# Sink attention: reciprocal sums widened on VectorE and turned inside the heads' banks, output casts a step later; fewer, larger loads at the start

## The chip, the cores and the metric

The kernel runs on one core of a Trainium2 chip. The metric is device time of one execution in microseconds, the median of three runs. A core has TensorE (PE; its weight loads are shown apart as PEld), VectorE (DVE), ScalarE (ACT), GpSimd (POOL) and SyncE (SP), which here only issues DMAs. Each engine works through its own queue in order; engines wait for one another by semaphores.

## The reference

Two blocks run one after the other on 256 tokens of width 1024, all in fp32. The first block has a gated feed-forward layer, a mixing layer with two kinds of attention, and a second feed-forward layer. The second block has two layers, each attention and then a feed-forward layer: the first with sliding-window attention with sinks (the *sink layer*), the second with stick-breaking attention. The sink layer is where most of the change lies; its core, cut:

```python
s = jnp.einsum('bqkgd,bskd->bkgqs', qb, kb).astype(jnp.float32) * scale
s = jnp.where(valid, s, -jnp.inf)
sink_col = jnp.broadcast_to(sink_logit, s.shape[:-1] + (1,))
p = jax.nn.softmax(jnp.concatenate([s, sink_col], axis=-1), axis=-1)[..., :-1]
o = jnp.einsum('bkgqs,bskd->bqkgd', p.astype(vb.dtype), vb)
```

So each query's exponentials are divided by their sum, the sink's own exponential included, over 16 heads of 64 features.

## The kernel before

Activations lie with features on partitions and 256 tokens along the free dimension. Every large matrix product is made of three matmuls on rounded halves: a high part (a cast to fp32r, `h`) and a low part (the rest, `l`), for the weights and for the activations. Weights come in blocks of 16 tiles of 128x128 (1 MB) into `raw`; ScalarE casts four tiles at a time to `wh` (L218), VectorE subtracts to `wl` (L226), and `W.step` lets one such quarter go after every four tiles of matmuls (`mm3`, L278 to L280). All other work is written as generators in a list of hooks: `pump()` lets each hook go one step and then calls `W.step`. So a step is twelve matmuls of 256 columns and whatever the hooks put into the queues in between; while an out projection waits for heads that are not ready, `pump()` is called with no matmuls in between.

**The start.** SP issues eight pairs of loads (L300, L302): a chunk of x (128 KB, called x0 to x7 here) and four weight tiles (256 KB, w0 to w7), then the rest of the weights and the constants. For each pair, ScalarE makes `xgh` (L843), the square `sq` (L335) and the cast `wh`, VectorE the low parts `xgl` (L846) and `wl`, and TensorE runs twelve matmuls on it. Eight fp32 matmuls on ones (L315), two passes each, run before the first load is there.

**The sink layer.** `soft_heads` takes heads in pairs; `run_heads` keeps up to three pairs going and starts one every second step at most. In the sink layer a pair goes: step 0, scores on TensorE (L697) and masked minimum on VectorE (L709); step 1, four exponentials on ScalarE with their sums (L718); step 2, reciprocal of the 2x2 sums on VectorE (`rs`, L723) and its spread to 64 columns for each head on GpSimd (`rw`, L727); step 3, three transposes for each head (`turn`, L739, copied to `pt` by ScalarE, L741), then two transposes of `rw` and a copy (`over_features`, L756, `rf`, L759); step 5, values (`weigh`, L749), the product `y` with `rf` on VectorE (L795) and the cast to `yh` on ScalarE (L797); step 6, the low part `yl` on VectorE (L799); step 7, the pair is marked ready for the out projection. PSUM banks for all of this come from `at_ps`, four in turn; an allocation waits until the bank four before it has been read. Beside it `operand` normalizes and rotates q and k, with transposes (L1114), copies to `qT` (L1120) and several GpSimd operations for each.

Of the kernel before, what the change touches and what calls it, by code (L numbers as in the profile page):

```python
# [11 lines left out]
F32 = mybir.dt.float32  # L12
# [7 lines left out]
S = 256  # L20
DC = 8
# [143 lines left out]
def hybrid_two_block_kernel(ctx: ExitStack, tc: tile.TileContext, x, w, ada, vecs, rows, pos, consts,  # L165
                            masks, out):
    nc = tc.nc
# [9 lines left out]
    def nm(s):  # L177
        count[0] += 1
        return f"{s}_{count[0]}"
# [4 lines left out]
    def at_ps(shape):  # L184
        return pp.tile(shape, F32, tag="at", bufs=4, name=nm("at"))
# [74 lines left out]
    W = Stream()  # L260
# [22 lines left out]
    xT = xp.tile([128, DC, S], F32, name="xT")  # L283
# [12 lines left out]
    for i in range(2):  # L296
        W.raw[i] = wp.tile([128, 16, 128], F32, tag="raw", bufs=W.RAW, name=nm("raw"))
    W.loaded = 2
    for kc in range(DC):
        nc.sync.dma_start(xT[:, kc], x[:, kc * S:(kc + 1) * S])  # L300
        i, t = divmod(4 * kc, 16)
        nc.sync.dma_start(W.raw[i][:, t:t + 4], w[i, :, 128 * t:128 * t + 512].rearrange("p (t c) -> p t c", t=4))  # L302
    W.load(3, 4)
    W.load(W.RAW, 2)
    nc.sync.dma_start(V[:, 8:], vecs[:, 8:])
# [3 lines left out]
    ident = C[:, C_ID:C_ID + 128]  # L309
# [1 line left out]
    ones = cp.tile([128, 128], F32, name="ones")  # L311
    nc.vector.memset(ones, 1.0)
    warm = at_ps([128, 128])
    for _ in range(8):
        nc.tensor.matmul(warm, lhsT=ones, rhs=ones, start=True, stop=True)  # L315
    mean_col = cp.tile([128, 1], F32, name="mean_col")
    nc.vector.memset(mean_col, 1.0 / D)
# [333 lines left out]
    def pause(n):  # L651
        for _ in range(n):
            yield

    def soft_heads(pool, n_heads, n_parts, part, y_h, y_l, ready, sink=None, gate=lambda j: True,
# [6 lines left out]
        cut = 128 + (sink is not None)  # L662
# [5 lines left out]
        def one(c):  # L668

            js = (2 * c, 2 * c + 1)  # L670
# [12 lines left out]
            u, lo, sums = {}, {}, {}  # L683
            both = pool.tile([128, 2, 2], F32, tag="sm", bufs=6, name=nm("sm"))
# [7 lines left out]
            for g in range(n_parts):  # L692
                p = {j: at_ps([128, 384]) for j in js}
# [25 lines left out]
                                         bias=lo[j][:, 2 * g + tt:2 * g + tt + 1],  # L719
                                         scale=-1.0, accum_out=sums[j][:, tt:tt + 1])  # L720
            yield from pause(gaps[0])
            rs = pool.tile([128, 2, 2], F32, tag="rs", bufs=6, name=nm("rs"))
            nc.vector.reciprocal(rs, both)  # L723
            if sink is not None:
                wide_rs = [pool.tile([128, 2, 64], F32, tag="rw", bufs=6, name=nm("rw")) for _ in range(2)]
                for tt in range(2):
                    nc.gpsimd.tensor_copy(wide_rs[tt], rs[:, tt].unsqueeze(2).to_broadcast([128, 2, 64]))  # L727
            if sink is None:
                for j in js:
                    for tt, sl in ((0, slice(0, 128)), (1, slice(cut, cut + 256))):  # L730
# [4 lines left out]
            def turn(j, g):  # L735

                ps = at_ps([128, 384])
                for at, a in ((0, 0), (128, cut), (256, cut + 128)):
                    nc.tensor.transpose(ps[:, at:at + 128], u[j][:, g, a:a + 128], ident)  # L739
                pt = pool.tile([128, 384], F32, tag="pt", bufs=6, name=nm("pt"))  # L740
                nc.scalar.copy(pt, ps)  # L741
                return pt

            def weigh(g, pts):
                for i in range(2):
                    for j in js:
                        v = part(j, g)[2][i]
                        oh = o[64 * (j % 2):64 * (j % 2) + 64, 128 * i:]
                        nc.tensor.matmul(oh, lhsT=v, rhs=pts[j][:, 256 * i:256 + 128 * i], start=g == 0 and i == 0,  # L749
                                         stop=g == n_parts - 1 and i == 1)  # L750

            def over_features():

                ps = at_ps([128, S])
                for tt in range(2):
                    nc.tensor.transpose(ps[:, 128 * tt:128 * tt + 128], wide_rs[tt].rearrange("p h e -> p (h e)"),  # L756
                                        ident)
                t = pool.tile([128, S], F32, tag="rf", bufs=3, name=nm("rf"))
                nc.scalar.copy(t, ps)  # L759
                return t  # L760

            pts = None
            for g in range(n_parts + 1):
                while not values():
                    yield
                if pts is not None:
                    if g == 1:
                        o = (at_ps if sink is not None else mm_ps)([128, S])
                    weigh(g - 1, pts)
                if g < n_parts:  # L770
                    if last is not None and pending:
                        pending.pop(0)()
                    pts = {j: turn(j, g) for j in js}
                    if sink is not None:
                        rf = over_features()
                    if last is not None:
                        break
                    yield from pause(gaps[2])
            if last is not None:
# [7 lines left out]
                o = None  # L787
# [4 lines left out]
                return  # L792
            if sink is not None:
                y = pool.tile([128, S], F32, tag="y", bufs=3, name=nm("y"))
                nc.vector.tensor_mul(y, o, rf)  # L795
                o = y
            nc.scalar.copy(y_h[:, c], o)  # L797
            yield
            nc.vector.tensor_sub(y_l[:, c], o, y_h[:, c])  # L799
            yield  # L800
            ready.add(c)

        pending, last = [], n_heads // 2 - 1 if merged else None
        return run_heads(n_heads // 2, one, gate, spacing, most)


# [34 lines left out]
    for d in range(DC):  # L841
# [7 lines left out]
        i, t = divmod(4 * d, 16)  # L849
# [25 lines left out]
    with ExitStack() as mix:  # L875
# [73 lines left out]
        with tc.tile_pool(name="merge", bufs=1) as gp:  # L949
# [5 lines left out]
            for d in range(DC):  # L955
# [6 lines left out]
                for kc in range(4):  # L962
                    t = 4 * (d % 4) + kc
                    mm3(pb, bh[:, t], bl[:, t], ybh[:, kc], ybl[:, kc], kc == 0, kc == 3)
                for kc in range(2):
                    t = 2 * d + kc
# [200 lines left out]
    with ExitStack() as mix:  # L1167
# [122 lines left out]
        name = "wqkv_b_2"  # L1290
# [74 lines left out]
```

## Time and profile before

| | |
|---|---|
| median of three runs | 1174.76 us (1174.7 to 1174.78) |
| profiled execution | 1174.54 us |
| its span | 1172.7 us |
| TensorE busy | 1160.4 us (99%) |
| VectorE busy | 946.5 us (81%) |
| ScalarE busy | 627.3 us (53%) |
| GpSimd busy | 125.3 us (11%) |
| DMA | 251.72 MB, mean 215 GB/s |

Times inside the profile count from the start of its span. The start of the kernel is 0 to 17 us; the heads of the sink layer run from about 605 to 672 us. Busy shares are means over the whole span; what an edit is worth is read from the stretch it lies in, and there from which wait ends last.

### The profile page before, as it was taken

What the parts mean: (1) busy time and instruction counts of PE and PEld (TensorE: products, weight loads), DVE (VectorE), ACT (ScalarE), POOL (GpSimd) and SP (SyncE); (2) the same over time, 40 slices, a digit from 0 to 9 for tenths busy, and PEclk for the clock granted to TensorE, in tenths of its full rate; (3) what the DMA queues carried; (4) which work ended last, traced back from release to release, by engine and by line L of the source; (5) the groups of instructions that cost most, each with busy time, mean ns of one, the idle gap of its engine ahead of it and who ended that gap; (6) DMA issues with size and microseconds to landing.
All of it is one profiled execution on the core that took longest, in us unless ns stands there. A gap on an engine that the chain in (4) does not pass through costs nothing.

```text
span 1172.7 us, 24635 instructions
## 1 busy us (share of the span) xinstructions
PE 1160.4 (99%) x9762; PEld 1129.9 (96%) x9762; DVE 946.5 (81%) x1991; ACT 627.3 (53%) x1344; POOL 125.3 (11%) x174
## 2 busy tenths in 40 slices
PE   9999999999999999999999999999999999999998
PEld 8999999999899999999997899999999999999998
DVE  7999987565667999999876699999969677888652
ACT  6545544455546554554467765554448666555531
POOL 2000011120202200001256220000110002000000
PEclk9999999999999999999999999999999999999999
DMA  8887756534334777876551277777654436765450
GB/s 318 325 299 276 269 210 209 213 113 176 114 139 149 259 275 306 334 277 233 180 187 72 83 284 296 307 270 278 249 191 149 164 122 215 258 215 181 170 200 20
DMA packets 45762, 251.72 MB, mean 215 GB/s; under 512 B 5328, under 2 KB 7888, under 8 KB 22224
## 3 DMA queue, kind: packets, MB, share of 16 engines
q1 hardware_dynamic: 45072, 248.78, 58.1%
q8 instruction: 77, 1.26, 0.4%
q10 hardware_dynamic: 576, 1.38, 0.4%
q14 instruction: 37, 0.30, 0.1%
HBM read 249.09 MB, written 1.05 MB: 213 GB/s over the span
## 4 chain that ended last, share of the span: by engine, by line
PE 90%; DVE 5%; ACT 2%; POOL 1%; issue 1%; DMA 0%; SPq 0%; DVEq 0%; ACTq 0%; POOLq 0%
PE mm L278 26%; PE mm L279 26%; PE mm L280 26%; DVE wl L226 2%; PE mm L594 1%; PE mm L596 1%; PE mm L595 1%; PE at L279 1%; PE at L280 1%; PE at L278 1%; PE at L697 1%; PE at L739 1%; ACT wells L718 1%; PE mm L749 1%; PE at L1233 1%
## 5 line engine op out<-in xcount | busy, mean ns | idle before, releaser
L218 ACT CAST wh<-raw 128x512 fp32r<-128x512 f32 (+1 forms) x749 | 420.4, 615 | 241.9 <-issue 117.6
L226 DVE TENSOR_TENSOR wl<-raw,wh 128x512 fp32r<-128x512 f32 (+1 forms) x749 | 502.4, 704 | 52.5 <-ACT wh L218 51.8
L278 PE MATMUL mm<-xgh,wh 128*128 128x256 f32 (+1 forms) x1712 | 486.1, 284 | 0.3 <-DVE sh L1037 0.2
L280 PE MATMUL mm<-xgh,wl 128*128 128x256 f32 (+1 forms) x1712 | 482.9, 282 | 0.0
L279 PE MATMUL mm<-xgl,wh 128*128 128x256 f32 (+1 forms) x1712 | 482.1, 282 | 0.0
L278 PEld LDWEIGHTS mm<-xgh,wh 128*128 128x128 f32 x1712 | 322.9, 189 | 4.3 <-issue 3.6
L279 PEld LDWEIGHTS mm<-xgl,wh 128*128 128x128 f32 x1712 | 324.0, 189 | 0.0
L280 PEld LDWEIGHTS mm<-xgh,wl 128*128 128x128 f32 x1712 | 323.1, 189 | 0.0
L279 PE MATMUL mm<-al,wh 128*128 128x256 f32 x704 | 197.0, 280 | 0.0
L278 PE MATMUL mm<-ah,wh 128*128 128x256 f32 x704 | 196.8, 280 | 0.0
L280 PE MATMUL mm<-ah,wl 128*128 128x256 f32 x704 | 196.4, 279 | 0.0
L278 PEld LDWEIGHTS mm<-ah,wh 128*128 128x128 f32 x704 | 132.3, 188 | 0.1
L279 PEld LDWEIGHTS mm<-al,wh 128*128 128x128 f32 x704 | 132.1, 188 | 0.0
L280 PEld LDWEIGHTS mm<-ah,wl 128*128 128x128 f32 x704 | 131.8, 187 | 0.0
L338 POOL TENSOR_TENSOR ssq<-ssq,sq 128x256 f32<-128x256 f32 x56 | 47.1, 846 | 669.0 <-ACT sq L335 668.1
L429 DVE SCALAR_TENSOR_TENSOR acc<-ada,cs,acc 128x1024 f32<-128x1024 f32 x84 | 107.6, 1281 | 1.1 <-DMA ada<-in_ada 0.5
L335 ACT ACTIVATE sq<-xT 128x256 f32<-128x256 f32 x49 | 19.9, 411 | 80.8 <-DVE xT L555 72.3
L491 DVE TENSOR_TENSOR tu<-mm,rB 128x256 f32<-128x256 f32 x80 | 33.5, 419 | 20.6 <-PE mm L280 20.5
L504 ACT CAST ah<-a 128x256 fp32r<-128x256 f32 x88 | 35.3, 405 | 23.3 <-DVE a L502 16.7
L497 ACT ACTIVATE sg<-tg,bb 128x256 f32<-128x256 f32 x44 | 22.3, 508 | 32.4 <-DVE bb L495 31.8
L506 DVE TENSOR_TENSOR al<-a,ah 128x256 fp32r<-128x256 f32 x88 | 36.6, 420 | 1.9 <-ACT ah L504 1.9
L280 PE MATMUL at<-xgh,wl 128*128 128x256 f32 (+1 forms) x128 | 36.7, 287 | 0.8 <-DVE wl L226 0.6
(227 smaller groups left out, 1552.6 us busy)
## 6 DMA issues: line engine op xcount, KB each, us to landing
raw<-in_w SPq DMA_DIRECT2D x183, 1024.0 KB, 5.4
ada<-in_ada SPq DMA_DIRECT2D x96, 512.0 KB, 4.8
raw<-in_w SPq DMA_DIRECT2D x12, 256.0 KB, 5.3
xT<-in_x SPq DMA_DIRECT2D x8, 128.0 KB, 4.6
raw<-in_w SPq DMA_DIRECT2D x2, 512.0 KB, 8.2
out<-xT SPq DMA_DIRECT2D x8, 128.0 KB, 2.1
M<-in_masks ACTq DMA_DIRECT2D x1, 768.0 KB, 4.3
Mstick<-in_masks ACTq DMA_DIRECT2D x1, 386.0 KB, 3.0
```

Source lines behind the costliest of these rows:

```text
L218: nc.scalar.copy(h[:, part], self.raw[i][:, part])
L226: engine.tensor_sub(l[:, part], self.raw[i][:, part], h[:, part])
L278: nc.tensor.matmul(ps, lhsT=lh, rhs=rh, start=start, stop=False)
L279: nc.tensor.matmul(ps, lhsT=lh, rhs=rl, start=False, stop=False)
L280: nc.tensor.matmul(ps, lhsT=ll, rhs=rh, start=False, stop=stop)
L335: nc.scalar.activation(t, src, AF.Square, scale=scale)
L338: nc.gpsimd.tensor_add(self.ssq, self.ssq, t)
L429: nc.vector.scalar_tensor_tensor(self.acc, raw, self.cs[:, kc:kc + 1], self.acc, op0=ALU.mult, op1=ALU.add)
L491: nc.vector.tensor_mul(tu, ps[1][:, :S], norm.r)
L497: nc.scalar.activation(sg, tg, AF.Silu, bias=bb[:, 0:1] if shift else 0.0)
L504: nc.scalar.copy(ah[:, c], a)
L506: nc.vector.tensor_sub(al[:, c], a, ah[:, c])
```

## The change

At the start, the eight pairs of loads become five: chunks 0 and 1 singly, then 2 and 3, 4 and 5, 6 and 7 together, x and weights alike. Ten instead of eight matmuls on ones run ahead. In the sink layer one VectorE reciprocal reads the 2x2 sums with a broadcast and writes them 64 columns wide for each head and half (`wide_rs`, 128x256); GpSimd's two copies are gone. `turn_two` puts a head's three transposes and one transpose of `wide_rs` into one 512-column bank and copies the bank at once; `rf` is the last quarter of these copies. The cast to `yh` moves from step 5 to step 6, right ahead of the low part. Other attention layers keep their path.

```diff
-    for kc in range(DC):
-        nc.sync.dma_start(xT[:, kc], x[:, kc * S:(kc + 1) * S])
+    for kc, n in ((0, 1), (1, 1), (2, 2), (4, 2), (6, 2)):
+        nc.sync.dma_start(xT[:, kc:kc + n], x[:, kc * S:(kc + n) * S].rearrange("p (c s) -> p c s", c=n))
         i, t = divmod(4 * kc, 16)
-        nc.sync.dma_start(W.raw[i][:, t:t + 4], w[i, :, 128 * t:128 * t + 512].rearrange("p (t c) -> p t c", t=4))
+        nc.sync.dma_start(W.raw[i][:, t:t + 4 * n],
+                          w[i, :, 128 * t:128 * (t + 4 * n)].rearrange("p (t c) -> p t c", t=4 * n))
...
-    for _ in range(8):
+    for _ in range(10):
         nc.tensor.matmul(warm, lhsT=ones, rhs=ones, start=True, stop=True)
...
-            rs = pool.tile([128, 2, 2], F32, tag="rs", bufs=6, name=nm("rs"))
-            nc.vector.reciprocal(rs, both)
-            if sink is not None:
-                wide_rs = [pool.tile([128, 2, 64], F32, tag="rw", bufs=6, name=nm("rw")) for _ in range(2)]
-                for tt in range(2):
-                    nc.gpsimd.tensor_copy(wide_rs[tt], rs[:, tt].unsqueeze(2).to_broadcast([128, 2, 64]))
+            if sink is None:
+                rs = pool.tile([128, 2, 2], F32, tag="rs", bufs=6, name=nm("rs"))
+                nc.vector.reciprocal(rs, both)
+            else:
+                wide_rs = pool.tile([128, 2, 2, 64], F32, tag="rw", bufs=4, name=nm("rw"))
+                nc.vector.reciprocal(wide_rs, both.unsqueeze(3).to_broadcast([128, 2, 2, 64]))
...
-            def over_features():
-
-                ps = at_ps([128, S])
-                for tt in range(2):
-                    nc.tensor.transpose(ps[:, 128 * tt:128 * tt + 128], wide_rs[tt].rearrange("p h e -> p (h e)"),
-                                        ident)
-                t = pool.tile([128, S], F32, tag="rf", bufs=3, name=nm("rf"))
-                nc.scalar.copy(t, ps)
-                return t
+            def turn_two():
+
+                pt = pool.tile([128, 2, 512], F32, tag="pt2", bufs=3, name=nm("pt2"))
+                for j in js:
+                    ps = at_ps([128, 512])
+                    for at, a in ((0, 0), (128, cut), (256, cut + 128)):
+                        nc.tensor.transpose(ps[:, at:at + 128], u[j][:, 0, a:a + 128], ident)
+                    nc.tensor.transpose(ps[:, 384:512], wide_rs[:, j % 2].rearrange("p h e -> p (h e)"), ident)
+                    nc.scalar.copy(pt[:, j % 2], ps)
+                return {j: pt[:, j % 2, :384] for j in js}, pt[:, :, 384:512]
...
-                    pts = {j: turn(j, g) for j in js}
-                    if sink is not None:
-                        rf = over_features()
+                    if sink is None:
+                        pts = {j: turn(j, g) for j in js}
+                    else:
+                        pts, rf = turn_two()
...
-                nc.vector.tensor_mul(y, o, rf)
+                nc.vector.tensor_mul(y.rearrange("p (t q) -> p t q", t=2), o.rearrange("p (t q) -> p t q", t=2), rf)
                 o = y
-            nc.scalar.copy(y_h[:, c], o)
-            yield
+                yield
+                nc.scalar.copy(y_h[:, c], o)
+            else:
+                nc.scalar.copy(y_h[:, c], o)
+                yield
             nc.vector.tensor_sub(y_l[:, c], o, y_h[:, c])
```

## Rows read from the trace of the kernel before

**Rows 1.** The page, busy time of each engine, share of the span, instructions

```profile
PE 1160.4 (99%) x9762; PEld 1129.9 (96%) x9762; DVE 946.5 (81%) x1991; ACT 627.3 (53%) x1344; POOL 125.3 (11%) x174
```

**Rows 2.** What TensorE waited for, whole span: us in total, times, longest

```profile
PE at L756 <- POOL rw L727: 2.0, 4, 0.9
...
PE at L739 <- ACT qT L1120: 0.7, 1, 0.7
```

**Rows 3.** Timeline of TensorE at the start: start us, us, instruction, [idle before <-releaser]

```profile
1.05 3.69 PE L315 MATMUL at<-ones 128*128 128x128 f32 x16 [1.05 <-DVE mhalf L319]
...
5.50 0.38 PE L278 MATMUL at<-xgh,wh 128*128 128x256 f32 x1 [0.76 <-ACT wh L218]
...
14.82 0.38 PE L280 MATMUL at<-xgh,wl 128*128 128x256 f32 x1 [0.39 <-DVE wl L226]
```

**Rows 4.** Timeline of SP's DMA issues at the start: issues of w2 and w3

```profile
3.06 0.43 SPq L302 DMA_DIRECT2D raw<-in_w  x1
...
4.01 0.43 SPq L302 DMA_DIRECT2D raw<-in_w  x1
```

**Rows 5.** DMA issues, KB each, median us to landing: w2, w3, block 3's halves

```profile
raw<-in_w SPq DMA_DIRECT2D x1, 256.0 KB, 5.2
...
raw<-in_w SPq DMA_DIRECT2D x1, 256.0 KB, 5.3
...
raw<-in_w SPq DMA_DIRECT2D x2, 512.0 KB, 8.2
```

**Rows 6.** Timeline of ScalarE at the start: the casts of w2 and w3

```profile
8.30 0.62 ACT L218 CAST wh<-raw 128x512 fp32r<-128x512 f32 x1 [0.59 <-DMA raw<-in_w]
...
9.55 0.60 ACT L218 CAST wh<-raw 128x512 fp32r<-128x512 f32 x1
```

**Rows 7.** Stretches: length, busy (instructions) of PE, PEld, DVE, ACT, POOL, PEclk, DMA, GB/s

```profile
5.00:10.00 5.00, 4.14 (x28) 3.56 (x29) 3.47 (x7) 4.36 (x11) 1.94 (x3) 1.00 0.90 301
10.00:15.00 5.00, 4.61 (x37) 4.32 (x37) 4.86 (x7) 4.55 (x12) 3.55 (x5) 1.00 0.89 246
```

**Rows 8.** VectorE's groups, 598 to 672 us: busy us, mean ns, idle before

```profile
L1100 DVE TENSOR_TENSOR ht<-at,R 128x256 f32<-128x256 f32 x9 | 3.4, 419 | 2.5 <-ACT hsq L1099 1.8 <-POOL rw L727 0.7
...
L1103 DVE TENSOR_SCALAR hss<-hss 128x4 f32<-128x4 f32 x9 | 1.5, 171 | 0.3
L723 DVE RECIPROCAL rs<-sm 128x4 f32<-128x4 f32 x8 | 1.4, 176 | 9.4 <-ACT wells L718 9.3
...
L1036 DVE COPY shb<-mm 128x1 f32<-128x1 f32 x8 | 1.2, 150 | 0.4 <-PE mm L280 0.4
```

**Rows 9.** ScalarE's groups of the same stretch

```profile
L741 ACT COPY pt<-at 128x384 f32<-128x384 f32 x16 | 6.8, 479 | 2.3 <-PE at L739 2.3
...
L797 ACT CAST yh<-y 128x256 fp32r<-128x256 f32 x8 | 3.2, 406 | 9.8 <-DVE y L795 9.8
L759 ACT COPY rf<-at 128x256 f32<-128x256 f32 x8 | 3.1, 385 | 0.0
```

**Rows 10.** Timelines of TensorE and of ScalarE around 640 us

```profile
638.38 0.91 PE L739 MATMUL at<-C,wells 128*128 128x128 f32 x6
...
643.65 0.48 PE L756 MATMUL at<-C,rw 128*128 128x128 f32 x2
...
639.67 0.40 ACT L797 CAST yh<-y 128x256 fp32r<-128x256 f32 x1 [1.40 <-DVE y L795]
...
641.08 0.41 ACT L718 ACTIVATE wells<-wells,lo 128x129 f32<-128x129 f32 x1
...
642.85 0.63 ACT L1120 ACTIVATE qT<-at 128x256 f32<-128x256 f32 x2
```

**Rows 11.** The same two timelines around 660 us

```profile
656.93 0.87 PE L739 MATMUL at<-C,wells 128*128 128x128 f32 x6
...
662.13 0.33 PE L756 MATMUL at<-C,rw 128*128 128x128 f32 x1 [0.42 <-POOL rw L727]
...
657.50 0.41 ACT L797 CAST yh<-y 128x256 fp32r<-128x256 f32 x1 [1.73 <-DVE y L795]
```

## The prediction

> **What bounds the kernel now.** I read the busy shares first: TensorE is busy for 1160.4 of 1172.7 us, VectorE for 81%, ScalarE for 53% [rows 1]. The chain of work that ended last says the same: nearly all of it is matmuls. So time can only be won or lost where TensorE itself stands still, and a stall added or removed there is passed on whole, because the matmuls behind it follow one another without slack. Third, the list of what TensorE waited for, over the whole span [rows 2]: the sink layer stands in it with 2.0 us in four waits for GpSimd's copy rw, and 0.7 us for a bank that ScalarE still reads. Last the timeline of the start, where the waits are for the first casts and low parts [rows 3]. These are fractions of a microsecond each; no large gain is on offer, and 0.2% (2.35 us) is about what a measurement of this kernel can tell from no change.
>
> **The profiled execution** took 1174.54 us, span 1172.7 us; the median of the runs shown is 1174.76, 0.22 us more. I make the sum against 1174.54 and add the 0.22 at the end.
>
> **Part 1, the loads at the start.** Up to the second weight piece nothing changes: x0, w0, x1, w1 are issued in the same order, and the first real matmul waits for the cast of w0 and starts at 5.50 [rows 3]. Two more warm-up matmuls: the 16 passes of eight take 3.69 us from 1.05, 0.23 a pass [rows 3]; four more end 0.92 us later at that price, at 5.66. The hole in front of the first matmul is 0.76 us [rows 3], so they cost between 0 and 0.16 us; I take 0, since the 3.69 holds the start and the tail of a row of passes too, and a further pass costs less than 0.23.
>
> The third pair is where it decides. Today w2 (256 KB) is issued at 3.06 [rows 4] and lands 5.2 us later [rows 5], at 8.26; ScalarE's cast of it starts at 8.30 after 0.59 us of waiting for that DMA [rows 6]. From there the path is tight: VectorE, which makes the low parts, is busy for 4.86 of the 5 us from 10 to 15 [rows 7], and TensorE waits for it at the end of that row of splits again (0.39 us before 14.82) [rows 3]. So a later w2 moves everything behind it, one for one. After the change x2 and x3 come as one transfer of 256 KB and w2 and w3 as one of 512 KB, issued when x2 and w2 are. The cast of w2 then waits for the last byte of w3. Bounds: not before w2 lands today, 8.26 (gain excluded: more bytes stand ahead of the same event), and not later than w3 lands today, 4.01 + 5.3 = 9.31 [rows 4, 5], because up to there the queue carries the same 1536 KB and today's is issued a microsecond later. That is +0 to +1.05 us. I take +0.7, nearer to the upper end, since the slowest of the 16 engines sets a landing and the same bytes lie before it. Behind it nothing new is late: w3 is then there; w4 to w7 come in steps of 768 KB for two pairs, and at the 301 GB/s of 5 to 10 us [rows 7] that is 2.6 us, against 2.5 us that ScalarE takes for two pairs (8.30 to 9.55 for one [rows 6]). Fewer issues also free SP's queue: sixteen issues become ten. This moves block 2 and the small constants forward, which TensorE does not wait for today, so it is worth nothing.
>
> **Part 2, the sink layer.** Per pair of heads (eight pairs) the change removes a reciprocal of four elements (176 ns [rows 8]), two GpSimd copies and a 256-column ScalarE copy (385 ns [rows 9]); it adds a VectorE reciprocal of 256 elements and makes two copies 512 columns wide instead of 384. The transposes stay eight. The copies: 384 columns take 479 ns, 256 take 385 [rows 9], so 0.73 ns a column and 0.57 us for 512; two of them 1.15 against 2 x 0.479 + 0.385 = 1.34 us. ScalarE wins 0.19 us a pair. The wide reciprocal is not in this trace. Lower bound: it streams like the other 128x256 operations, 0.42 us (ht, 419 ns [rows 8]). Upper bound: a copy of one element takes 150 ns and the reciprocal of four 176 [rows 8]; if those 26 ns are all due to three more elements, 8.7 ns each, 256 take 0.18 + 252 x 8.7 = 2.4 us. Nearer is TENSOR_SCALAR on four elements, 171 ns [rows 8]: 5 ns over four is 1.2 ns each on top, and 0.73 us. I take 0.42, since an operation of the same size that is no reciprocal explains all but these 5 ns.
>
> The Trainium skill speaks against this step: its page "VectorE: DVE Perf Modes", section "First, the fixed hardware budget", says that the reciprocal is an iterative divide with a repeat count of 8. If that means eight passes for each element, the instruction would come out near the 2.4 us of the upper bound and the sum as in rival B; the four-element row, 5 ns above its neighbour, does not bear it out.
>
> What goes: TensorE's waits for rw, 2.0 us [rows 2]; the longest, 0.9, stands around 640, the last, 0.42, before 662.13 [rows 11], the others at the first and last pair. What takes their place: the reciprocal is queued on VectorE behind something new. Today the cast of y is queued on ScalarE at once behind y, and ScalarE stands waiting for it (1.40 us before 639.67 [rows 10], 1.73 before 657.50 [rows 11]). Afterwards cast and low part come in the next step together, ahead of the reciprocal of the pair two further on. On ScalarE the cast then lies behind that pair's four exponentials (1.77 us, 641.08 to 642.85 [rows 10]) and a weight cast or two qT copies; on VectorE the low part waits for the cast, and the reciprocal waits behind the low part.
>
> I follow it at the two places where TensorE has nothing else to do. *Around 640:* the transposes of that pair start at 638.38 [rows 10], or about 0.5 earlier with the first pairs' waits gone (637.9); ScalarE no longer waits for y, 0.6 until the first wide copy can start, 1.0 until the exponentials start, 1.8 for them, 0.6 for two qT copies [rows 10], 0.4 each for the cast, the low part and the reciprocal, 0.6 for the five transposes that are left, 5.8 in all: 643.7. Today the same transposes end at 644.13 (643.65 + 0.48 [rows 10]). Gain 0.4 us, of the 0.9 and 0.7 that stood there. *Around 660:* today 656.93 (transposes begin) to 662.46 is 5.5 us, the next matmul following at once [rows 11]. Afterwards the same terms hold, with one weight cast (0.6, as in [rows 6]) in place of the qT copies: 5.8 us. So 0.3 of the 0.4 goes back. Sum of the stage: -0.1 us. Its range: -2.0 (all waits for rw go and nothing replaces them) to +1.1 (the reciprocal at 0.73 in both places, 0.6 together, and a second weight cast of 0.6 ahead of the cast).
>
> The later cast itself costs the projection nothing: the pair's mark of readiness stays in the same step, and where the last pair's result is first used some 24 matmuls lie between.
>
> **Sum:** 1174.54 + 0.7 - 0.1 + 0.22 = 1175.4 us.
>
> **The rivals.**
> - *A, faster:* ScalarE, no longer waiting for y (9.8 us in the stage [rows 9]), runs so far ahead that the cast is done before VectorE asks for it; then the waits for rw (2.0) and for the qT bank (0.7) [rows 2] go, and the third load lands where w2 does: 1174.76 - 2.7 = 1172.1. It decides from the point where the cast of one pair ends before the exponentials two pairs on. Against it: these stand ahead of it in ScalarE's order. Chance 0.13.
> - *B, slower, the reciprocal iterates:* 2.4 instead of 0.42 us stands on the path at both places, 2 x 1.98 = 4.0 on top of the forecast: 1179.4. It decides from about 1.3 us an instruction. Against it: the four-element row. Chance 0.11.
> - *C, slower, the third load is late:* a 512 KB piece of this kernel has been seen to take 8.2 us to landing [rows 5]; from 3.06 that is 11.3, 3.0 later than today: 1174.76 + 3.0 - 0.1 = 1177.7. Against it: those pieces stood behind seven others. It decides from a landing 2.5 us later. Chance 0.07.
>
> **How the numbers follow.** Forecast 0.69, A 0.13, B 0.11, C 0.07. The forecast lies in the band of 1172.4 to 1177.1, so within 0.2% has 0.69, faster 0.13, slower 0.18. The forecast's own range is 1172.8 (0 and -2.0) to 1176.9 (+1.05 and +1.1). The range reaches towards A and takes in C: 1172.3 to 1177.8; B and about half of A, which lies just outside, are left out, 0.18 together.
>
> **What would show it.** The cast of w2 starts between 8.3 and 9.3, later than today, with a DMA named as what it waited for, and the row of splits behind it is later by as much. The 128x256 reciprocal takes 0.4 to 0.7 us. No TensorE wait names rw; new ones name the reciprocal, of up to 2 us before the last pair's transposes; VectorE's low part waits for the cast, up to 1.5 us each, and ScalarE's 9.8 us of waiting for y are gone. Wrong if w2 and w3 land at 8.3 or earlier, if the start gains, or if the transposes around 662 stand without a wait for the reciprocal.

## The result, and the profile after

The changed kernel takes **1185.36 us** (median of 4 runs, 1184.47 to 1187.48) against 1174.77 of before: a ratio of 1.0090, 95% interval 1.0078 to 1.0102. It is 10.6 us slower. The prediction was 1175.4 us with no measurable change; its range ended at 1177.8. The profiled execution took 1187.48 us, span 1185.7, the slowest of the four; the terms below that come from its trace are those of this execution. Of the later cast alone, one of the experiments below, one execution ran at a granted clock of 0.655 and took 1589 us; it is left out, and with it the only trace of that version.

The wide reciprocal stands in VectorE's groups of the sink layer, 598 to 690 us (line, engine, operation, shapes and count; busy us, mean ns; idle before), where [rows 8] had the four-element one, with the low part below it:

```profile
L728 DVE RECIPROCAL rw<-sm 128x256 f32<-128x256 f32 x8 | 14.0, 1748 | 3.2 <-ACT wells L719 3.0
...
L805 DVE TENSOR_TENSOR yl<-y,yh 128x256 fp32r<-128x256 f32 x8 | 3.9, 484 | 6.0 <-ACT yh L801 6.0
```

It takes 1748 ns, ten times the 176 of [rows 8] and four times what the sum put in. The low part waits 6.0 us for the cast. ScalarE's groups of the same stretch, for [rows 9]:

```profile
L761 ACT COPY pt<-at 128x512 f32<-128x512 f32 x16 | 9.0, 587 | 13.0 <-PE at L760 13.0
...
L801 ACT CAST yh<-y 128x256 fp32r<-128x256 f32 x8 | 3.2, 404 | 2.6 <-DVE y L798 2.6
```

The 512-column copy is at 587 ns as worked out (0.57), and the wait for y fell from 9.8 to 2.6 us. But ScalarE stands 13.0 us for TensorE's transposes of rw, because TensorE itself stands ahead of them (2.3 us for transposes in [rows 9]). What TensorE waited for, whole span, for [rows 2]:

```profile
PE at L760 <- DVE rw L728: 8.7, 4, 3.3
PE at L278 <- ACT wh L218: 1.6, 1, 1.6
```

The four waits for GpSimd's copies, 2.0 us, became four waits for VectorE's reciprocal, 8.7 us, the longest 3.3 us, ahead of 650.60. All four in the timeline of TensorE (start us, us, instruction, [idle before <-releaser]), with the transposes just ahead of the longest:

```profile
626.47 0.33 PE L760 MATMUL at<-C,rw 128*128 128x128 f32 x1 [1.87 <-DVE rw L728]
...
643.94 0.33 PE L760 MATMUL at<-C,rw 128*128 128x128 f32 x1 [0.73 <-DVE rw L728]
...
646.72 0.55 PE L759 MATMUL at<-C,wells 128*128 128x128 f32 x3
650.60 0.33 PE L760 MATMUL at<-C,rw 128*128 128x128 f32 x1 [3.33 <-DVE rw L728]
...
672.12 0.47 PE L760 MATMUL at<-C,rw 128*128 128x128 f32 x1 [2.79 <-DVE rw L728]
```

ScalarE's timeline ahead of 650.60:

```profile
644.31 0.59 ACT L761 COPY pt<-at 128x512 f32<-128x512 f32 x1 [1.70 <-PE at L760]
645.28 0.59 ACT L761 COPY pt<-at 128x512 f32<-128x512 f32 x1 [0.39 <-PE at L760]
645.77 0.41 ACT L719 ACTIVATE wells<-wells,lo 128x129 f32<-128x129 f32 x1
...
647.54 0.39 ACT L801 CAST yh<-y 128x256 fp32r<-128x256 f32 x1
```

and VectorE's:

```profile
645.06 0.42 DVE L798 TENSOR_TENSOR y<-at,pt 128x256 f32<-128x256 f32 x1
647.96 0.92 DVE L805 TENSOR_TENSOR yl<-y,yh 128x256 fp32r<-128x256 f32 x1 [2.48 <-ACT yh L801]
648.80 1.74 DVE L728 RECIPROCAL rw<-sm 128x256 f32<-128x256 f32 x1
```

Read from below: the transposes of rw wait for a reciprocal of 1.74 us, which stands behind the low part, which stands 2.48 us for a cast that lies behind four exponentials although its input y is there at 645.48. That is the order the prediction followed, with another duration at its end.

A second loss was not in the prediction at all. Stretches of the changed kernel (length; busy and instructions of PE, PEld, DVE, ACT, POOL; granted clock; DMA share; GB/s):

```profile
627.00:630.00 3.00, 3.00 (x16) 3.00 (x15) 2.73 (x9) 2.47 (x6) 2.69 (x7) 0.50 0.00 0
651.00:654.00 3.00, 3.00 (x15) 2.02 (x14) 0.65 (x3) 2.25 (x5) 0.00 (x0) 0.50 0.03 5
672.00:677.50 5.50, 5.38 (x25) 5.38 (x26) 1.96 (x5) 2.00 (x4) 0.00 (x0) 0.50 0.01 3
```

and the first of them in the kernel before:

```profile
627.00:630.00 3.00, 3.00 (x31) 2.50 (x27) 2.58 (x14) 1.89 (x7) 1.88 (x3) 1.00 0.00 0
```

The granted clock is at 0.50 (1.2 GHz, the lower of its two levels) in the three stretches, in each of which TensorE had stood for rw just before or at its start (1.87 us before 626.47, 3.33 before 650.60, 2.79 before 672.12). TensorE is busy in them, but with half the instructions: 16 in 3 us instead of 31. Before, the clock is at 1.00 there. At the start the clock fell too in this execution: 0.76 over 10 to 15 us, where [rows 7] have 1.00.

Instructions that both kernels have start 2.0 us later at 600 us (the start's share), 13.15 later at 690 (the sink layer's share is 11.1), and 13.15 later to the end: nothing else differs.

At the start, two rows of ScalarE's timeline: the high part of x2, and the cast of w2 that answers to [rows 6]:

```profile
8.43 0.51 ACT L849 ACTIVATE xgh<-xT,V 128x256 fp32r<-128x256 f32 x1 [1.61 <-DMA xT<-in_x]
...
10.10 0.62 ACT L218 CAST wh<-raw 128x512 fp32r<-128x512 f32 x1 [0.85 <-DMA raw<-in_w]
```

and TensorE's, for [rows 3]:

```profile
5.34 0.55 PE L278 MATMUL at<-xgh,wh 128*128 128x256 f32 x1
...
10.77 0.39 PE L278 MATMUL at<-xgh,wh 128*128 128x256 f32 x1 [1.57 <-ACT wh L218]
```

The cast of w2 moved from 8.30 to 10.10 us. ScalarE stood for the merged x2 and x3 first, 1.61 us, which the prediction did not count, and then for the merged weights. The two more warm-up matmuls cost nothing (first real matmul at 5.34, 5.50 before).

### The profile page after: what moved, and what is told of

The parts are those of the page before. It is cut to its first block, busy times and chain, and to the rows that moved or that the text cites. A ratio compares the mean times of both kernels' runs of the same rounds, so it can differ in the third digit from the quotient of the medians.

```text
span 1185.7 us, 24587 instructions
## 1 busy us (share of the span) xinstructions
PE 1167.3 (98%) x9766; PEld 1137.3 (96%) x9766; DVE 958.3 (81%) x1991; ACT 626.8 (53%) x1336; POOL 121.0 (10%) x158
## 3 DMA queue, kind: packets, MB, share of 16 engines
HBM read 249.09 MB, written 1.05 MB: 211 GB/s over the span
## 4 chain that ended last, share of the span: by engine, by line
PE 90%; DVE 5%; ACT 2%; POOL 1%; issue 1%; DMA 1%; SPq 0%; ACTq 0%; DVEq 0%; POOLq 0%
PE mm L278 26%; PE mm L279 26%; PE mm L280 25%; DVE wl L226 2%; PE mm L595 1%; PE mm L597 1%; PE mm L596 1%; PE at L279 1%; PE at L280 1%; PE at L278 1%; PE at L698 1%; ACT wells L719 1%; DVE rw L728 1%; PE mm L750 1%; PE at L740 1%
## 5 line engine op out<-in xcount | busy, mean ns | idle before, releaser
L278 PE MATMUL mm<-yh,wh 128*128 128x256 f32 x128 | 38.8, 304 | 0.0
L278 PE MATMUL at<-xgh,wh 128*128 128x256 f32 (+1 forms) x128 | 37.1, 290 | 1.6 <-ACT wh L218 1.6
```

The lines of the kernel that those rows point to most:

```text
L278: nc.tensor.matmul(ps, lhsT=lh, rhs=rh, start=start, stop=False)
```

## The experiments

The theory to be tested: the reciprocal has a price per element; it makes TensorE stand, and a standing TensorE loses its clock as well. The rivals: the broadcast read is slow, not the reciprocal; the later cast is the loss; the loss sits at the start. Times of runs are compared with runs of the kernel before on the same chip, whose median moved between 1174.55 and 1175.07 us from one group of runs to the next.

**The two halves apart.** The first is the kernel before with the merged loads and ten warm-up passes, the second the changed kernel with the old start.

> The kernel before with the merged first loads and the ten warm-up passes alone; the sink layer is as before. The trace of the changed kernel stands about 2.0 us behind that of before from 40 us on, so the sum of the start is +2.0 us (1176.8) if the two halves of the change add up. Theory S: w2, now in one transfer with w3, lands later, its cast by ScalarE moves from 8.30 to about 10.1 us, TensorE stands for 1.6 us, and the granted clock falls to its lower level (1.2 GHz) for one stretch just behind it, so that work which ran at 2.4 GHz takes up to 1.7 us longer. Expected: the same cast at about 10.1 us, a stretch at the granted clock 0.5 within 12 to 16 us, +1.7 to +2.3 us. Rival: the prediction's start term alone (+0.7 us, no fall of the clock), with the rest of the 2 us made by the sink layer's code: 1175.5. Second rival: nothing at the start costs anything once the sink layer is as before: 1174.8.

> The changed kernel with the start of the kernel before; only the sink layer's part of the change is left in. In the changed kernel's profiled execution the sink layer stood for some 11 us and the start for 2, in its median run for 10.6 us in all. Expected: +8.5 to +11 us (1183.3 to 1185.8), the reciprocals of 128x256 at about 1.75 us each, and stretches at the granted clock 0.5 behind TensorE's longest waits around 627, 651 and 672 us. If the sink layer's part were worth the -0.1 us of the prediction, it would be 1174.7. If the two halves only cost together (a start that shifts the later schedule), it would be well under 1183.

Measured: the start alone 1175.42 against 1174.97, ratio 1.0003 (0.9994 to 1.0012); the sink layer alone 1184.51, ratio 1.0076 (1.0061 to 1.0091). The loss is the sink layer's, +9.5 us. The start's expectation missed: its clock stayed at 1.00, and while the trace shows +1.0 us from 100 us on, the times show +0.45: the first rival's 1175.5 came. The changed kernel once more beside them:

> The changed kernel once more, beside the others on one chip. Its two parts alone gave 1175.4 (the start) and 1184.5 (the sink layer). If they add up, it takes 1184.9 to 1185.5. If the start's part does more together with the sink layer's than alone, it takes 1186 or more. In its first profiled execution the clock fell also at 12.4 us, which it did not in that of the start's part alone; if that fall belongs to the kernel, it shows again and the start costs 2 us, and if it comes only in some executions, it may be gone with the start at +1.0.

It took 1184.77, ratio 1.0089 (1.0072 to 1.0106), the start at +1.1 us in its trace with the clock at 1.00 there. So the clock's fall at 12 us comes in some executions only.

**What a reciprocal costs.** Ten instructions whose results nobody reads, in the second stage (the lines that make their tiles, and the yields, are left out here):

```diff
+        for n in (1, 4, 16, 64, 128, 256, 512):
+            nc.vector.reciprocal(t[:, :n], xT[:, 0:2].rearrange("p c s -> p (c s)")[:, :n])
+        b4 = four.unsqueeze(2).to_broadcast([128, 4, 64])
+        nc.vector.reciprocal(t[:, :256].rearrange("p (a b) -> p a b", a=4), b4)
+        nc.vector.tensor_copy(t[:, :256].rearrange("p (a b) -> p a b", a=4), b4)
+        nc.vector.tensor_copy(t[:, :256], xT[:, 0])
```

> The kernel before with ten more VectorE instructions amid the second stage, whose results nobody reads: reciprocals of 1, 4, 16, 64, 128, 256 and 512 neighbouring elements a partition, one of 256 that reads four elements by broadcast, a copy of 256 by the same broadcast, and a plain copy of 256. Theory T (a price per element of the reciprocal): 0.18 us for 4 elements and 1.75 us for 256 make 6.2 ns an element over a fixed 0.15 us, so about 0.25 (16), 0.55 (64), 0.95 (128), 1.75 (256), 3.3 us (512), the same with and without broadcast, and copies at 0.3 to 0.45 us. Rival R1 (the broadcast is slow): the plain reciprocal of 256 at 0.4 to 0.7 us, and both broadcast instructions at 1.7 us. Since the time of this kernel includes these extra instructions, only their durations count.

VectorE's groups of that stretch:

```profile
L863 DVE RECIPROCAL tsz<-xT 128x512 f32<-128x512 f32 x1 | 3.3, 3349 | 0.0
L863 DVE RECIPROCAL tsz<-xT 128x256 f32<-128x256 f32 x1 | 1.8, 1753 | 0.0
L866 DVE RECIPROCAL tsz<-tfour 128x256 f32<-128x256 f32 x1 | 1.7, 1748 | 0.0
...
L863 DVE RECIPROCAL tsz<-xT 128x64 f32<-128x64 f32 x1 | 0.5, 544 | 0.0
L870 DVE COPY tsz<-xT 128x256 f32<-128x256 f32 x1 | 0.3, 300 | 0.0
L868 DVE COPY tsz<-tfour 128x256 f32<-128x256 f32 x1 | 0.3, 297 | 0.0
L863 DVE RECIPROCAL tsz<-xT 128x16 f32<-128x16 f32 x1 | 0.2, 246 | 0.0
L863 DVE RECIPROCAL tsz<-xT 128x4 f32<-128x4 f32 x1 | 0.2, 170 | 0.0
L863 DVE RECIPROCAL tsz<-xT 128x1 f32<-128x1 f32 x1 | 0.2, 166 | 0.0
```

From 16 to 512 elements it is (3349 - 246) / 496 = 6.26 ns an element over some 146 ns. Read by broadcast or side by side, 256 take the same (1748, 1753), and so do the copies (297, 300). Each duration is the one that the theory named; the broadcast rival falls.

**The same widening without the wide reciprocal** (the line that makes the tile `rs` is left out here).

```diff
-                nc.vector.reciprocal(wide_rs, both.unsqueeze(3).to_broadcast([128, 2, 2, 64]))
+                nc.vector.reciprocal(rs, both)
+                nc.vector.tensor_copy(wide_rs, rs.unsqueeze(3).to_broadcast([128, 2, 2, 64]))
```

> As the kernel with the sink layer's part alone, but the reciprocal is taken on four sums (128x4) and VectorE widens the result with one broadcast copy of 128x256; turning inside the heads' banks and the later cast stay. Theory T (the reciprocal's price is per element, about 6 to 7 ns each, and nothing else in the sink layer costs): the pair of instructions takes 0.18 + about 0.42 us in place of 1.75, TensorE's long waits for it go, the clock stays at its upper level, and the time is 1174.3 to 1175.5. Rival R1 (the broadcast read or the write of 256 numbers is what is slow, whatever the operation): the copy takes about 1.7 us and the time stays at 1183 to 1186. Rival R2 (the later cast, or the turning inside the heads' banks, is the loss): the copy is quick, and the time still is above 1179.

Measured 1176.88, ratio 1.0014 (1.0004 to 1.0023). VectorE's two groups in the sink layer:

```profile
L729 DVE COPY rw<-rs 128x256 f32<-128x256 f32 x8 | 2.7, 341 | 0.3
...
L727 DVE RECIPROCAL rs<-sm 128x4 f32<-128x4 f32 x8 | 1.4, 172 | 4.8 <-ACT wells L718 4.7
```

and what TensorE waited for, in an execution that took 1175.04 us with the clock at 1.000:

```profile
PE at L761 <- DVE rw L729: 3.6, 2, 2.0
```

0.51 us in place of 1.75 takes back 7.6 of the 9.5 us. Not all: the time lies above the theory's 1175.5 and below the second rival's 1179. Three of its ten executions kept the clock at 1.000 and took 1175.0 to 1176.1; the others, at 0.997 to 0.999, took 1176.6 to 1177.8.

**The waits apart from the clock.** Useless passes keep TensorE busy in its four longest waits:

```diff
+                    for _ in range({1: 8, 3: 3, 4: 15, 7: 13}.get(c, 0) if j % 2 == 0 else 0):
+                        nc.tensor.matmul(ps[:, 384:512], lhsT=ones, rhs=ones, start=True, stop=True)
```

> The kernel with the sink layer's part alone, and in it useless TensorE passes (128x128 of ones, overwritten by what follows) ahead of the transposes of the widened sums, in the four places where TensorE waited longest for them (8, 3, 15 and 13 passes of about 0.21 us). It waits as long, but TensorE is busy while it waits. In the profiled execution of the sink layer's part alone (+9.65 us over the layer), the granted clock over 640 to 690 us is short of 1.00 by 5.1 us in all (0.86 over 10, 0.80 over 10, 0.96 over 12 and 0.93 over 18 us). Theory T (long waits, then the clock): with TensorE kept busy the clock stays at 1.00 over the layer and the time is 4 to 5 us less: 1179 to 1181. Rival: the lower clock is not caused by the standing of TensorE, and costs nothing: 0.5 behind it as before, and 1183 to 1186.

Measured 1180.17, ratio 1.0043 (1.0028 to 1.0058), granted clock 1.000 in each of the four executions. Two stretches (columns as above) without the passes:

```profile
640.00:650.00 10.00, 5.89 (x36) 3.66 (x34) 5.04 (x13) 5.71 (x17) 8.13 (x13) 0.86 0.00 0
650.00:660.00 10.00, 10.00 (x72) 9.09 (x71) 7.19 (x24) 4.70 (x16) 0.00 (x0) 0.80 0.31 107
```

and with them:

```profile
640.00:650.00 10.00, 9.39 (x80) 7.62 (x77) 5.80 (x15) 5.42 (x17) 8.75 (x15) 1.00 0.01 2
650.00:660.00 10.00, 10.00 (x86) 8.75 (x86) 8.21 (x25) 7.07 (x25) 0.00 (x0) 1.00 0.28 106
```

More work, 4.3 us less time: of the sink layer's 9.5 us, 4.3 are work done at the lower clock, and 5.1 (1180.17 against 1175.07) are the waits themselves, with whatever the passes overran them by. TensorE's waits for rw had grown by more, 8.4 us in the trace of the sink layer alone against 2.0 before, but other waits of before are gone there, such as the 0.7 for the qT bank [rows 2]. The same on the version with the copy (8 and 6 passes in its two waits):

> The version with the broadcast copy on VectorE and the later cast (1176.9 us, with a granted clock of 0.997 to 1.000; 1175.0 to 1176.1 in its three executions at 1.000), with useless TensorE passes (8 and 6 of 128x128) in the two places where TensorE waited for the widened sums by 2.0 and 1.5 us. Theory (the loss is the lower clock behind the two waits, not the waits): the clock stays at 1.000 in all executions, and it takes 1175.0 to 1176.0. Rival (the waits alone are the loss): as without the passes, 1176.5 to 1177.5.

Measured 1174.87 against 1174.55, ratio 1.0002 (0.9993 to 1.0011), the clock at 1.000 in nine of ten executions. That is just under the theory's range. The loss falls from 1.9 to 0.3 us: nearly all that was left of it there was the clock's.

**The later cast.** First alone in the kernel before, then undone beside the wide reciprocal, and undone beside the copy:

```diff
                 o = y
-            nc.scalar.copy(y_h[:, c], o)
-            yield
+                yield
+                nc.scalar.copy(y_h[:, c], o)
+            else:
+                nc.scalar.copy(y_h[:, c], o)
+                yield
```

The first run has this edit, the other two its reverse.

> The kernel before with one edit: the cast of the sink layer's output a step later. With the broadcast copy on VectorE the later cast took 1176.9 us and the earlier one 1175.0, and in the slower one TensorE's longest wait for the widened sums was 2.0 us in place of 1.1. Theory: the later cast by itself lengthens what the low part, and behind it the next reciprocal, wait for on VectorE, so TensorE waits longer around 643 us and the clock falls in some executions: 1176 to 1177.5. Rival (the prediction: a later cast takes 0.4 us off ScalarE's waiting around 640 and is free otherwise): 1174.5 to 1175.1.

> The kernel with the sink layer's part alone, but ScalarE's cast of the output stands a step earlier, where the kernel before had it. Theory T: the cast's place isn't what costs; the wide reciprocals still take 1.75 us and TensorE still waits for them: 1183 to 1186. Rival R2 (the later cast is the loss, since what comes behind a pair ends a step later): it comes near the kernel before, under 1179.

> The four-element reciprocal with VectorE's broadcast copy, turning inside the heads' banks, and the cast a step earlier as in the kernel before. The version with the copy and the later cast took 1176.9 us, and 1175.0 in an execution whose clock stayed at 1.00; VectorE stood 6.5 us in it for the casts. Theory: the later cast costs up to 1 us here, so 1174.5 to 1176.5. Rival (the prediction's): the earlier cast makes ScalarE stand for y as it did before (9.8 us), so it is slower than with the later cast: 1177 to 1179.

Alone: median 1175.36 of nine executions against 1174.55, ratio 1.0004 (0.9995 to 1.0014), not to be told from nothing; the theory's 1176 to 1177.5 missed. Undone beside the wide reciprocal: 1186.11, ratio 1.0089 (1.0074 to 1.0104), 0.1 us over the theory's range and no gain either, though the low part's wait is all but gone from VectorE's groups:

```profile
L801 DVE TENSOR_TENSOR yl<-y,yh 128x256 fp32r<-128x256 f32 x8 | 3.4, 420 | 0.5 <-ACT yh L799 0.5
```

TensorE's wait for the reciprocal stays:

```profile
PE at L759 <- DVE rw L727: 7.0, 4, 2.2
```

Undone beside the copy: 1174.96, ratio 0.9998 (0.9989 to 1.0008), where the later cast gave 1.0014. TensorE's longest wait for rw is 1.1 us then, not 2.0, and the clock is not lost (0.999 or 1.000 in nine of ten executions; the tenth stands at 0.949 and took 1175.6 us, no longer than others, so that one figure stays unexplained). So the later cast seems to cost where it lengthens a wait of TensorE enough. The rival that it was the main loss falls.

**GpSimd's widening with the rest of the change** (the four-element reciprocal and two GpSimd copies, turning inside the heads' banks, later cast):

> The sink layer's part with the four-element reciprocal on VectorE and the widening by two GpSimd copies, as in the kernel before; turning inside the heads' banks and the later cast stay. It leaves of the change only what isn't the wide reciprocal. Theory: like the version with VectorE's copy and the later cast, 1176.9, and up to 0.5 us more for GpSimd's longer way: 1176.5 to 1177.5. Rival: the turning inside the heads' banks saves ScalarE's third copy and brings it down to the kernel before: 1174.5 to 1175.5.

1177.43, ratio 1.0022 (1.0012 to 1.0031). TensorE waits more for GpSimd than in the kernel before, 5.2 us against 2.0 [rows 2], as its list of waits shows:

```profile
PE at L762 <- POOL rw L730: 5.2, 4, 1.9
```

Turning inside the heads' banks with the later cast doesn't win even without the wide reciprocal; since the later cast alone is not measurable and the turning with the earlier cast (beside VectorE's copy) isn't either, it should be the two together. That is argued from three versions; which of their waits does it was not taken apart.

**The sums' transposes last** (copy, earlier cast, the sums' transposes behind those of both heads):

```diff
+                ps = {j: at_ps([128, 512]) for j in js}
+                for j in js:
+                    for at, a in ((0, 0), (128, cut), (256, cut + 128)):
+                        nc.tensor.transpose(ps[j][:, at:at + 128], u[j][:, 0, a:a + 128], ident)
+                for j in js:
+                    nc.tensor.transpose(ps[j][:, 384:512], wide_rs[:, j % 2].rearrange("p h e -> p (h e)"), ident)
+                    nc.scalar.copy(pt[:, j % 2], ps[j])
```

> The version with the broadcast copy on VectorE and the earlier cast (1175.0 us against 1175.1 of before), with the two transposes of the widened sums behind the transposes of both heads' weights, so that three more passes (about 0.8 us) lie ahead of TensorE's wait for the copy. That wait was 1.1 and 0.7 us. Theory (each stall of TensorE is passed on whole): most of 1.8 us goes, 1173.5 to 1174.8, the first version under the kernel before. Rival: the wait is for the exponentials of both heads, and ScalarE's copy of the first head comes later by the same, so the gain is taken back: 1174.7 to 1175.5.

1174.57 against 1174.55, ratio 1.0000 (0.9991 to 1.0008). Of TensorE's wait for rw 0.3 us are left, but others stand in the list:

```profile
PE at L760 <- ACT qT L1125: 0.7, 1, 0.7
PE at L760 <- DVE ht L1105: 0.6, 1, 0.6
...
PE at L760 <- DVE lo L709: 0.6, 1, 0.6
...
PE at L762 <- DVE rw L729: 0.3, 1, 0.3
```

The time lies in the theory's range, but the theory's point, a version under the kernel before, did not come: on this chip the kernel before takes 1174.55. As the rival said, the gain is taken back; most of the wait only changed its name. It is the quickest version found and no quicker than the kernel before.

**The start once more**, with more rounds, and its loads without the two more warm-ups:

> The kernel before with the whole of the start's part (merged loads, ten warm-up passes), timed once more, with more rounds. Theory S: the third pair, merged, lets ScalarE's cast of w2 start about 1.5 us later, of which some 1 us reaches the end: +0.5 to +1.2 us. Rival: nothing of it reaches the end: within 0.3 us of before.

> The kernel before with the merged loads alone, eight warm-up passes as before. The first real matmul started no later with ten passes (5.34 us against 5.50 in the profiled executions), so Theory S expects the same as with the whole of the start's part, +0.5 to +1.2 us, and the cast of w2 at about 10 us. Rival (the warm-ups are what costs): as the kernel before, within 0.3 us.

The whole start: 1175.18 against 1174.91, ratio 1.0002 (0.9993 to 1.0011), where the rival had it. The loads alone: 1175.84, ratio 1.0007 (0.9998 to 1.0016), where Theory S had them. Neither can be told from nothing. The cast of w2 starts at 9.65 and 10.29 us, against 8.30 of [rows 6], and in the second trace TensorE waits for casts in two places:

```profile
PE at L278 <- ACT wh L218: 2.3, 2, 1.6
```

In that trace the clock fell at the start once more:

```profile
10.00:15.00 5.00, 3.82 (x18) 3.62 (x19) 3.95 (x7) 4.71 (x12) 3.08 (x4) 0.69 1.04 402
```

So of the five traces with merged loads it fell in the two in which TensorE stood longest for the cast of w2, 1.57 and 1.58 us, and not in the three in which it stood 0.87 to 1.05 us.

The two traces stand 0.7 and 2.1 us behind that of before, but traces of kernels with the unchanged start lie anywhere from 0.5 us ahead of it to 1.1 behind. The start's price is some 0.3 to 0.9 us and could not be told from nothing; nor could the two parts of it be told apart.

## Why the prediction was wrong

**The term that failed first is the wide reciprocal:** taken at 0.42 us, it measures 1.75. The two bounds, 0.42 and 2.4, hold the truth; the choice between them was wrong. It rested on the four-element reciprocal being 5 ns above a TENSOR_SCALAR of the same size [rows 8]. But four elements at 6.26 ns are 25 ns on a fixed part of 146, and the fixed parts of different operations differ by nearly as much (166 ns for the reciprocal of one element, 150 for the copy of one): a row that small says nothing on the price of an element. The upper bound, which compared it with a one-element copy, put 8.7 ns on an element and was the nearer one.

The Trainium skill's page "VectorE: DVE Perf Modes", section "First, the fixed hardware budget", has the reciprocal as an iterative divide with a repeat count of 8, and the prediction set it aside against the row. The runs agree in direction: 6.26 ns an element, where the 256-element copy at 300 ns, over the 150 of the one-element one [rows 8], has (300 - 150) / 255 = 0.59, a factor of about 11.

**The number of places was wrong too.** Both the forecast and rival B let the reciprocal count at two places, the fifth pair (around 640) and the eighth (around 660). There the two longest waits came, 3.33 us before 650.60 and 2.79 before 672.12. But two more pairs waited for it: the second, 1.87 us before 626.47, and the fourth, 0.73 before 643.94. In the kernel before, the second pair had no wait at all, and the fourth had the longest:

```profile
623.23 0.38 PE L756 MATMUL at<-C,rw 128*128 128x128 f32 x2
...
640.21 0.56 PE L756 MATMUL at<-C,rw 128*128 128x128 f32 x2 [0.92 <-POOL rw L727]
```

So a list of today's waits does not name the places where a longer instruction will be waited for. With the right duration rival B's own arithmetic gives 2 x (1.75 - 0.42) = 2.7 us; the waits alone measured 5.1.

**The clock was missing.** "A stall added or removed there is passed on whole" holds for the stall; the work behind it also ran at 1.2 GHz, for more than 3 us at a time, another 4.3 us. Nothing in the trace of before shows it, since its waits in the layer are at most 0.9 us and the clock is 1.00 there. With both, the sum closes: 1174.8 + 0.3 to 0.9 (start) + 5.1 (waits) + 4.3 (clock) = 1184.5 to 1185.1, against the 1184.8 and 1185.4 measured. The 5.1 and 4.3 make up the sink layer's loss by the way they were measured; what the sum tests is that the two halves of the change add up.

The Trainium skill's page "TensorE: Matmul & The Clock Gate", section "HAM oscillation — how this bites in real kernels", tells of a kernel in which each wait between bursts of matmuls makes the next burst start at the lower clock. The traces agree in part, with waits for another engine in place of a transfer. The clock fell around the end of each of the six waits of 2.8 us and more in the two traces of the changed kernel and that of the sink layer alone, but not with every shorter one. With the sink layer alone TensorE stood 1.87 us before 624.81, as long as before 626.47 in the changed kernel, and kept its clock (first two stretches below). With the earlier cast beside the wide reciprocal it stood 2.20 us before 648.85, lost it, stood 2.20 us before 670.58, and kept it (third stretch):

```profile
624.50:627.00 2.50, 2.19 (x17) 1.90 (x18) 2.46 (x8) 1.84 (x6) 1.59 (x5) 1.00 0.00 0
627.00:630.00 3.00, 3.00 (x28) 2.21 (x27) 2.53 (x12) 2.01 (x6) 2.92 (x6) 1.00 0.00 0
...
672.00:677.50 5.50, 5.50 (x49) 5.05 (x48) 2.68 (x6) 3.28 (x7) 0.00 (x0) 1.00 0.00 0
```

What decides it in between, no run here shows.

**The walk around 650.** The order was right: cast behind the exponentials, low part behind the cast, reciprocal behind the low part. From the first wide copy (644.31) to the reciprocal's end (650.54) it is 6.2 us, where the prediction's terms give 1.0 + 1.8 + 0.6 + 3 x 0.4 = 4.6 up to there. The reciprocal is 1.3 of the difference, the low part 0.4 (0.84 until the reciprocal starts), the copies 0.5 (the second one stood 0.39 us for TensorE), and the qT copies, which came behind the cast, took 0.6 off.

**The cast's place.** The prediction read a gain from ScalarE's 9.8 us of waiting for y. That wait did fall, to 2.6 us, and bought nothing: ScalarE was not what TensorE waited for. The engine then stood for TensorE's transposes, 13.0 us.

**The start.** The mechanism was right and its bound wrong. The landing of w2 was to be no later than w3's today, 9.31; the cast started at 9.62 to 10.29 in the five traces with merged loads, and at 8.09 to 8.91 in ten with the loads of before. The bound held that the same bytes stand ahead of it. By 4.01 us the merged issues have handed over x0 to x5 and w0 to w5 (six times 128 + 256 KB, 2304 KB) where before it was four times, 1536, at the same rate (296 GB/s from 5 to 10 us, 301 in [rows 7]). That later transfers share the engines with earlier ones would explain it, but no run here takes it apart. What reached the end, 0.3 to 0.9 us, holds the 0.7 that the sum put in, which is partly luck: the cast came later than its bound, and less of it reached the end than the "one for one" of the prediction. The warm-ups at 0 were right.

**The rivals.** B named the mechanism, with a chance of 0.11 and less than half the loss (4.6 of 10.6 us). A fell: the waits for rw grew instead of going. C's landing of 11.3 did not come. The signs that were announced spoke clearly: a reciprocal above 0.7 us, waits for it above 2 us, and a cast of w2 behind 9.3.

## What to carry to other kernels

Price an instruction that works element by element from a row with many elements, or give the far bound the weight that it has; an instruction of four elements shows only its fixed part. Widen with a copy, not with the reciprocal (0.51 against 1.75 us here). Where TensorE is the bound, a wait of two or three microseconds can cost nearly twice what the waiting itself does (9.5 against 5.1 us here), because the work behind it may run at half the clock: test this by filling the wait with useless passes and reading the granted clock.

## What the runs showed of the hardware

- VectorE's reciprocal takes 146 ns and 6.26 ns an element (16 to 512 elements a partition, f32), whether it reads side by side or by broadcast; a copy of 256 takes 0.30 us both ways.
- TensorE's granted clock fell to 0.50 for more than 3 us around the end of each of six waits of 2.8 to 3.3 us, amid a stage that was busy before and after. With waits of 1.6 to 2.2 us it fell in some cases and not in others, within one execution too (2.20 us twice). Over the sink layer it stayed at 1.00 in the traces whose waits were at most 1.1 us. The kernel in whose trace the waits were 2.0 and 1.5 us had a mean clock under 1.000 in seven of ten executions, and its times spread over 2.9 us (1174.96 to 1177.84).
- Useless matmuls in the waits brought 1184.5 down to 1180.2 us.
- Merged, a transfer of 512 KB that was issued at 3.06 us held its first user up to 9.6 to 10.3 us; its first half by itself held it up to 8.1 to 8.9.
